# Plain products for the first two projections and the first output block, and other buffers around them, in a hybrid attention layer

## The chip, the cores and the metric

The kernel runs on one core of a Trainium2 chip. The core has engines that run side by side, each with its own queue of instructions that it takes strictly in order: TensorE (PE, matrix products; its weight loads are listed as PEld), VectorE (DVE), ScalarE (ACT), GpSimd (POOL) and SyncE (SP, which here only issues DMA transfers). Data move from the chip's main memory to SBUF by DMA; TensorE writes its sums to PSUM, which this kernel uses as eight banks of 128 x 512 fp32, each cut in two halves of 256 columns. The metric is device time in microseconds (us), lower is better.

## What is computed

One layer (`DEPTH = 1`) over 512 tokens with model width 2048, all in fp32:

```python
def reference(x, norm_g, w_in, q_norm_g, k_norm_g, rel_bias, w_out):
    h = rms_norm(x, norm_g)                                   # 512 x 2048
    proj = h @ w_in                                           # 512 x 8192
    qa, ka, va, ga, qb, kb, vb, gb = split(proj, 8 x 1024)
    ya = stick_breaking_attention(qa, ka, va)                 # 8 heads of 128
    yb = chunk_band_attention(qb, kb, vb, q_norm_g, k_norm_g, rel_bias)   # 8 heads of 128
    mixed = concat(ya * silu(ga), yb * silu(gb))              # 512 x 2048
    return x + mixed @ w_out
```

## The kernel before

**Units.** The first product (`h @ w_in`) is cut into 32 *units*: 8 groups of two heads (A groups: stick-breaking, B groups: chunk band), and for each group the four kinds q, k, v and gate. A unit is a 256 x 512 block of the projection, summed over the 2048 channels. The output product (`mixed @ w_out`) is cut into four blocks of 512 output columns, numbers 32 to 35 (`NU + q`), each in two halves `a = 0, 1` of the tokens.

**Seven products for eight.** Every block is a 2 x 2 block product. The kernel forms it with seven block products, Winograd's variant of Strassen's scheme: sums of weight blocks (s1 to s4), sums of token blocks (T1 to T4), seven products, and a combination afterwards. A block is built up in *steps*: a unit has four (each takes two channel blocks j, kk = 0 and 1), an output block has eight (one j each). A step of a unit is 7 x 2 x 3 = 42 matmuls, a step of an output block 7 x 2 halves x 3 = 42.

**Three matmuls for a product.** A fp32 value is split into a rounded high part and a remainder: ACT casts the high part (`xh`, `wh`, in fp32r), DVE subtracts it from the value (`xl`, `wl`). `three` (L374 to L376) then issues high x high, and the two mixed products.

**What comes ahead of a step.** Weights: `load` (L265) brings 512 KB by two transfers; `sums` makes s1 to s4 on DVE (L282 512 columns, L285 and L286 256 each); `split` casts on ACT (L298) and subtracts on DVE (L303) in two parts: part 0 is A11, s3, A12, A22 (1024 columns), part 1 is s1, s2, s4 (768). Each part has two buffers, so the cast for a step waits until the products of the step before last that use this part are done. Token blocks: `activations(j)` loads a block j and its partner (L341 to L343) into a home of two 128 x 1024 buffers, scales it by `norm_g` (L350), splits the raw 768 columns (L357, L358 with 768), forms T1 to T4 on DVE (L364, L366, L367) and splits them (L357, L358 with 1024). There are two homes: `cq`+`ck` for even j and `cv`+`cg` for odd j. They are also the buffers in which later the units' results q, k, v and gate lie. A home takes the next j only when all of this is done.

**The mixed heads.** The heads' results are stored to memory (`mixd`, L918) and staged again through the same two homes for the output product (L341 to L343 from `mixd`). In the second product the odd home (`cv`, `cg`) is free only when the last head's gate has been applied and stored, the even home when the last q and k have been read.

**Banks.** Units 2 to 31 rotate over banks 0 to 4, four banks each (`place`, `unit_banks`); unit 1 lies in banks 4 to 7. The output blocks use banks 0 to 3 for a = 0 and 4 to 7 for a = 1. Banks 5 to 7 (`SPARE`) serve the attention in between. A half of a bank may be written again when `combine` has read it: an ACT copy of the first two products to the tile `U` (L489), then DVE L508, L510, L513, L515, L530. There is one tile `U`, and `combine` holds it from L489 to L530.

**The order.** A planner in the program itself (`schedule`) writes down all instructions: it runs its own clock with an assumed cost for each instruction, and on each engine takes the ready instruction with the earliest due time. PE takes an attention step if one is ready, and else the next product of the list `program`. Its order is then fixed; on the chip every engine waits at the head of its queue for whatever its next instruction needs.

**Other names.** `R` (L649) is 1/rms of the tokens spread over partitions by eight small matmuls (L644); before, it is made in a spare bank that it gets when unit 1 has finished. `xs` (L612, L617) are the 16 loads and squares for it. `residual` adds x to an output tile by a POOL transfer and stores it; for the last block x is loaded ahead (`residual_load`, L570) and added on DVE (L524 to L526).

Of the kernel before, what the change touches and what calls it, by code (L numbers as in the profile page):

```python
# [36 lines left out]
ORDER = ("A11", "A12", "s3", "A22", "s2", "s1", "s4")  # L37
TOKENS = dict(A11=0, A12=1, s2=5, s3=4, s1=3, A22=6, s4=2)

PLACE = dict(A11=0, A12=1, s3=2, A22=3, s2=4, s1=5, s4=6)  # L40


SLOT = dict(A11=0, s3=1, A12=4, A22=5, s1=8, s2=9, s4=12)
# [4 lines left out]
def trunk_kernel(ctx: ExitStack, tc: tile.TileContext, xT, xn, wi, wqk, wo, ng, qg, kg, rel, out):  # L48

# [71 lines left out]
    class Op:  # L121
        def __init__(self, engine, cost, fn, due=None, lag=0.0):
            self.engine, self.cost, self.fn, self.lag = engine, cost, fn, lag
            self.due = due if callable(due) else (lambda d=clock[0] + LATE if due is None else due: d)
# [33 lines left out]
    def issue(engine, op):  # L158
        op.fn()
        busy[engine] = clock[0] + op.cost  # L160
        if engine == "SP":
            dma_free[0] = max(dma_free[0], clock[0] + op.cost) + op.lag / 330e3
            return dma_free[0] + 2.2
# [65 lines left out]

    for n, (u, r) in enumerate(steps_):  # L230
        if u < NU:
            put(n, 0, ORDER)
        elif u == NU and r < 2:

            if r == 0:
                for n_, a in ((n, 0), (n + 1, 0), (n, 1), (n + 1, 1)):
                    put(n_, a, ORDER)
        elif r == NJ - 1:
            for a in range(2):
                put(n, a, ORDER)  # L240
        else:
            for x in ORDER:
                for a in range(2):
                    put(n, a, (x,))
    at_part = {}
    for k, (n, x, a) in enumerate(program):
        at_part.setdefault((n, SLOT[x] // 8), k)
    last_use = {(n, SLOT[x] // 8): k for k, (n, x, a) in enumerate(program)}
    takes = [0.75 if steps_[n][0] < NU else 0.36 for n, x, a in program]
# [11 lines left out]
    def load(n):  # L261
        a, b = rows(n)
        t = wt_[n] = tmp([P, 14 * P], "wt", f"wt{n}", bufs=3)
        for i, x in enumerate((a, b)):
            sp.dma_start(t[:, 2 * i * H:2 * (i + 1) * H].rearrange("p (a b) -> p a b", b=H), x)  # L265
# [6 lines left out]
    def all_weights():  # L272
        for n in range(NS):
            yield lambda: n < 3 or ("split", n - 3, 0) in done and ("split", n - 3, 1) in done
            k0, k1 = at_part[n, 0], at_part[n, 1]
            yield Op("SP", 0.15, lambda: load(n), need(k0, 7), lag=P * 4096)
            spawn(sums(n, k0, k1), (0, n))
# [742 lines left out]
```

## Time and profile before

| | |
|---|---|
| median of 3 runs | 1028.09 us (1025.92 to 1030.35) |
| profiled execution | 1026.74 us, its span from first to last instruction 1025.0 us |
| granted TensorE clock, mean | 0.976 |
| PE busy | 938.8 us (92%), 7496 matmuls |
| DVE, ACT busy | 860.0 us (84%), 591.3 us (58%) |
| moved by DMA | 112.41 MB, mean 110 GB/s |

The profile lists for each engine when it was busy, what ended its idle times, and in which order things ran. A matmul's row has the modelled length of one matmul (about 0.28 us at full clock), while the next starts earlier; so a rate is read from a count over a stretch, not from the mean. The granted clock of a stretch is a share of full speed. The prediction cuts the execution into stages and reads each by what PE waited for there.

### The profile page before, as it was taken

The numbers are of one execution on the slowest core, as the hardware profiler recorded it, in microseconds if no ns is written. First come the engines' busy times: TensorE is split into PE (matmuls) and PEld (weight loads), VectorE is DVE, ScalarE is ACT, GpSimd is POOL, SyncE is SP. The second block draws the span as 40 slices with busy tenths as digits, with TensorE's granted clock in tenths as the row PEclk, the third lists the DMA queues.
The fourth block names the chain that finished last, engine by engine and source line by source line (L and its number), as shares of the span: only waits on it lengthen the run. The fifth ranks groups of instructions, "written<-read, shape, count | busy, mean of one in ns | idle before, by whom it ended". The sixth has DMA issues, their size and how long they took to land.

```text
span 1025.0 us, 19307 instructions
## 1 busy us (share of the span) xinstructions
PE 938.8 (92%) x7496; PEld 919.6 (90%) x7496; DVE 860.0 (84%) x1531; ACT 591.3 (58%) x1082; POOL 18.8 (2%) x61
## 2 busy tenths in 40 slices
PE   5689999999999999999999999999999839898996
PEld 4689999999999998999999899999999839798996
DVE  6999988888889878888898887989889958877764
ACT  8855774865467547745674675467577625333431
POOL 0000000000000000000000000000000000101000
PEclk9789999999999999999999999999999959999998
DMA  8632333223322332232233223322324344546361
GB/s 258 215 103 83 102 94 105 76 80 124 103 63 96 121 99 78 80 122 88 83 100 117 83 74 123 104 74 82 104 73 143 121 128 134 136 143 165 106 163 41
DMA packets 63883, 112.41 MB, mean 110 GB/s; under 512 B 7472, under 2 KB 11568, under 8 KB 63792
## 3 DMA queue, kind: packets, MB, share of 16 engines
q1 hardware_dynamic: 62064, 108.04, 32.9%
q0 software_dynamic: 1728, 3.15, 1.9%
q8 instruction: 58, 0.95, 0.4%
q14 instruction: 33, 0.27, 0.1%
HBM read 102.77 MB, written 8.39 MB: 108 GB/s over the span
## 4 chain that ended last, share of the span: by engine, by line
PE 74%; DVE 14%; ACT 5%; issue 3%; DMA 3%; SPq 1%; DVEq 0%; ACTq 0%
PE banks L374 24%; PE banks L375 23%; PE banks L376 23%; DVE wl L303 3%; ACT wh L298 2%; PE banks L838 2%; DVE U L513 2%; DVE wt L282 1%; DVE xl L358 1%; DMA wt<-in_wi 1%; PE banks L766 1%; DVE c L515 1%; DMA xcv<-in_xT 1%; ACT xh L357 1%; DVE wt L286 1%
## 5 line engine op out<-in xcount | busy, mean ns | idle before, releaser
L374 PE MATMUL banks<-xh,wh 128*128 128x256 f32 x1792 | 521.8, 291 | 32.4 <-ACT wh L298 11.8
L375 PE MATMUL banks<-xl,wh 128*128 128x256 f32 x1792 | 511.1, 285 | 8.4 <-DVE xl L358 8.4
L376 PE MATMUL banks<-xh,wl 128*128 128x256 f32 x1792 | 510.1, 285 | 1.0 <-DVE wl L303 1.0
L298 ACT CAST wh<-wt 128x1024 fp32r<-128x1024 f32 x320 | 300.6, 942 | 309.3 <-PE banks L375 171.3
L303 DVE TENSOR_TENSOR wl<-wt,wh 128x1024 fp32r<-128x1024 f32 x320 | 347.6, 1089 | 86.8 <-ACT wh L298 85.1
L374 PEld LDWEIGHTS banks<-xh,wh 128*128 128x128 f32 x1792 | 346.3, 193 | 39.4 <-DVE c L515 12.9
L375 PEld LDWEIGHTS banks<-xl,wh 128*128 128x128 f32 x1792 | 346.6, 193 | 10.4 <-DVE xl L358 10.1
L376 PEld LDWEIGHTS banks<-xh,wl 128*128 128x128 f32 x1792 | 346.5, 193 | 1.2 <-DVE wl L303 1.2
L374 PE MATMUL banks<-wh,xh 128*128 128x256 f32 x448 | 129.5, 289 | 30.0 <-ACT xh L357 15.0
L376 PE MATMUL banks<-wh,xl 128*128 128x256 f32 x448 | 128.7, 287 | 2.4 <-DVE xl L358 2.4
L282 DVE TENSOR_TENSOR wt<-wt 128x512 f32<-128x512 f32 x160 | 109.6, 687 | 25.0 <-DMA wt<-in_wo 16.2
L375 PE MATMUL banks<-wl,xh 128*128 128x256 f32 x448 | 128.3, 286 | 0.0
L374 PEld LDWEIGHTS banks<-wh,xh 128*128 128x128 f32 x448 | 87.6, 196 | 32.0 <-ACT xh L357 15.6
L376 PEld LDWEIGHTS banks<-wh,xl 128*128 128x128 f32 x448 | 87.5, 195 | 3.2 <-DVE xl L358 3.2
L375 PEld LDWEIGHTS banks<-wl,xh 128*128 128x128 f32 x448 | 87.7, 196 | 0.0
L285 DVE TENSOR_TENSOR wt<-wt 128x256 f32<-128x256 f32 x160 | 67.1, 421 | 2.2
L286 DVE TENSOR_TENSOR wt<-wt 128x256 f32<-128x256 f32 x160 | 67.3, 421 | 1.8
L489 ACT COPY U<-banks 128x512 f32<-128x512 f32 x40 | 23.2, 581 | 21.6 <-PE banks L376 13.7
L847 DVE TENSOR_TENSOR wtl<-banks,wth 128x128 fp32r<-128x128 f32 (+1 forms) x64 | 31.1, 486 | 4.0 <-ACT wth L846 3.6
L846 ACT CAST wth<-banks 128x128 fp32r<-128x128 f32 (+1 forms) x64 | 26.8, 423 | 10.8 <-POOL wtl L854 4.5
L838 PE MATMUL banks<-ident,W 128*128 128x128 f32 x160 | 28.4, 275 | 1.5 <-ACT W L744 1.2
L739 DVE TENSOR_TENSOR_SCAN W<-L,W 128x128 f32<-128x128 f32 (+3 forms) x32 | 26.3, 821 | 0.0
(123 smaller groups left out, 902.7 us busy)
## 6 DMA issues: line engine op xcount, KB each, us to landing
wt<-in_wi SPq DMA_DIRECT2D x256, 256.0 KB, 3.0
wt<-in_wo SPq DMA_DIRECT2D x64, 256.0 KB, 3.2
xs<-in_xn SPq DMA_DIRECT2D x16, 256.0 KB, 5.0
mixd<-c SPq DMA_DIRECT2D x16, 256.0 KB, 2.6
out<-co SPq DMA_DIRECT2D x16, 256.0 KB, 4.1
co<-in_xn POOLq DMA_DIRECT2D x12, 256.0 KB, 6.2
bias<-in_rel SPq DMA_DIRECT2D x8, 256.0 KB, 3.4
xcq<-in_xT SPq DMA_DIRECT2D x8, 128.0 KB, 3.3
```

The source lines that it names most:

```text
L282: yield DV(512, lambda: dve.tensor_tensor(out=some(t, 8, -7, 2), in0=some(t, 5, -5, 2), in1=some(t, 1, 0, 2), op=ALU.add), need(k0, 4))
L285: yield DV(256, lambda: dve.tensor_tensor(out=some(t, 9, 2), in0=some(t, 8, 2), in1=some(t, 0, 2), op=ALU.add), need(k1, 4))
L286: yield DV(256, lambda: dve.tensor_tensor(out=some(t, 12, 1), in0=some(t, 9, 2), in1=some(t, 4, 2), op=ALU.add), need(k1, 3.5))
L298: act.copy(x[0], t)
L303: yield DV(w, lambda: dve.tensor_tensor(out=l, in0=t, in1=h.bitcast(F32), op=ALU.subtract), need(k, 0.5))
L374: pe.matmul(o, lh, rh, start=start, stop=False, **kw)
L375: pe.matmul(o, lh, rl, start=False, stop=False, **kw)
L376: pe.matmul(o, ll, rh, start=False, stop=stop, **kw)
L739: yield Op("DVE", 0.08 + 2.1e-3 * w, lambda: dve.tensor_tensor_scan(out=W[:, ::-1], data0=L[:, ::-1], data1=W[:, ::-1], initial=0.0, op0=A ...
L838: pe.transpose(t[:, j * P:(j + 1) * P], src[:, j * P:(j + 1) * P], ident)
L846: yield AC(w, lambda: act.copy(th[:, blocks, :], tv))
L847: yield DV(w, lambda: dve.tensor_tensor(out=tl[:, blocks, :], in0=tv, in1=th[:, blocks, :].bitcast(F32), op=ALU.subtract))
```

## The change

Two tables replace the order and the placement: a step's products are now a list of (weight block, token block, target half). For units 0 and 1 (all four steps) and for output block 32 (all eight steps, `PLAIN_STEPS`), the list is `PLAIN`: the eight ordinary block products of the raw blocks. Such a block has four targets and two banks; its result needs no combination, only two ACT copies (`copied`). Its weights need no sums and no part 1. Weights of steps 0 and 1 are loaded and split in two halves.

Token block B12 is needed raw only for `PLAIN`; its split (`XB`, `xb`) lies in buffers that are idle at that time (`qk`, `wth`, `wtl`, `v`). The raw blocks are split in pieces (256, 256 for B12, 512 columns). Staging also makes T1 to T4 for the later blocks, in the same homes. For the mixed heads, odd j no longer wait for `cv` and `cg`: their home is the `qk` buffer, free when the last scores are done.

Output block 32 uses banks 4, 0 (a = 0) and 1, 3 (a = 1); the following ones 4, 0, 1, 2 and 3, 5, 6, 7. The second half's `combine` has a tile of its own (tag `bias`) in place of the shared `U`. `R` no longer waits for unit 1's banks. The loads of x for the last block (`residual_load`) come after step 1 of block 33 has begun. In the last block the store of the first half of the columns is spawned and no longer stands in the sequence. The planner's assumed costs of a product change a little (0.705 to 0.72, 0.355 to 0.36).

```diff
+WINOGRAD = (("A11", "B11", 0), ("A12", "B21", 1), ("s3", "T3", 2), ("A22", "T4", 3), ("s2", "T2", 4),
+            ("s1", "T1", 5), ("s4", "B22", 6))
+PLAIN = (("A11", "B11", 1), ("A11", "B12", 6), ("A21", "B11", 3), ("A21", "B12", 7),
+         ("A12", "B21", 1), ("A12", "B22", 6), ("A22", "B21", 3), ("A22", "B22", 7))
+ALONE = {1: 0, 6: 1, 3: 2, 7: 3}
+PLAIN_STEPS = 8
...
+    def plain(u, r):
+        return u < 2 or u == NU and r < PLAIN_STEPS
...
     for n, (u, r) in enumerate(steps_):
+        names = PLAIN if plain(u, r) else WINOGRAD
         if u < NU:
-            put(n, 0, ORDER)
-        elif u == NU and r < 2:
-            if r == 0:
-                for n_, a in ((n, 0), (n + 1, 0), (n, 1), (n + 1, 1)):
-                    put(n_, a, ORDER)
-        elif r == NJ - 1:
+            put(n, 0, names)
+        elif r in (0, NJ - 1):
...
+        if plain(*steps_[n]):
+            yield from split(n, 0, k)
+        else:
+            yield from sums(n, k, at_part[n, 1])
...
+        yield lambda: ((i < 1 or ("hi", having[part][i - 1], part) in done)
+                       and (i < 2 or position[0] > last_use[having[part][i - 2], part]))
...
         if mixed:
             g = j // 2 * 2
             yield lambda: (("store", g, j % 2) in done and ("store", g + 1, j % 2) in done
-                           and all(emptied(t_, NG - 1) for t_ in tags)
-                           and position[0] >= at_step[steps_.index((last, j // 2))] + NP)
+                           and position[0] > at_step[step_of[NU - 1, j // 2]] + 6)
+            yield lambda: all(emptied(t_, NG - 1) for t_ in STAGE[0]) if j % 2 == 0 else ("scores", 2 * NG - 1) in done
...
+        if mixed and j % 2:
+            rt = tmp([P, 2, 4 * H], "qk", f"x{j}{mixed}")
+            r, t = rt[:, 0, :], rt[:, 1, :]
...
+    def raw_split(j, mixed, r, k, x0, x1, names, h, l):
+        if h is None:
+            if mixed:
+                yield lambda: ("values", 2 * NG - 1) in done
+            h, l = xb(j, mixed)
+        s_ = r[:, x0 * H:x1 * H]
+        yield AC((x1 - x0) * H, lambda: act.copy(h, s_), need(k, 2.6))
+        yield DV((x1 - x0) * H, lambda: dve.tensor_tensor(out=l, in0=s_, in1=h.bitcast(F32), op=ALU.subtract), need(k, 0.5))
...
+    def unit_banks(u, a):
+        if alone(u):
+            return ((0, 1), (2, 3))[u] if u < NU else ((4, 0), (1, 3))[a]
+        if a:
+            return 3, 5, 6, 7
+        b = 4 * (sequence.index(u) - 1) if u < NU else 4
+        return [(b + i) % 5 for i in range(4)]
...
+    def copied(u, a):
+        v = view(u)
+        there = lambda *x: lambda: all(("product", u, y, a) in done for y in x)
+        c, t = yield from result(u, a)
+        for f, (x, y) in enumerate(((1, 6), (3, 7))):
+            yield there(x, y)
+            yield AC(512, lambda: act.copy(c[f], v(pair(u, a, x, y))), clock[0] + 1)
+            for z in (x, y):
+                del holder[place(u, a, z)]
+        yield from finish(u, a, t)
...
     def combine(u, a):
...
+        tag = "bias" if a else "U"
...
-        yield lambda: "U" not in done
-        done.add("U")
+        yield lambda: ("U", tag) not in done
+        done.add(("U", tag))
...
     def residual_load(a):
-        yield lambda: ("mix", NG - 1, 1) in done
+        yield lambda: position[0] >= at_step[step_of[NU + 1, 1]]
...
-    owner = {i: "unit 1" for i in SPARE}
+    owner = {}
```

**At the start, on DVE.** These are the first rows that DVE gets (behind a name stands a running number; `xcq00`, `xcv10` are blocks j = 0 and 1, `wt0`, `wt1` the weights of steps 0 and 1). Before:

```order
L364 TENSOR_TENSOR xck00_115<-xcq00_114 128x512
L366 TENSOR_TENSOR xck00_115<-xck00_115,xcq00_114 128x256
L358 TENSOR_TENSOR xl0_139<-xcq00_114,xh0_138 128x768
L367 TENSOR_TENSOR xck00_115<-xck00_115,xcq00_114 128x256
L282 TENSOR_TENSOR wt0_124<-wt0_124 128x2x2x128
L364 TENSOR_TENSOR xcg10_120<-xcv10_119 128x512
L358 TENSOR_TENSOR xl1_152<-xcv10_119,xh1_151 128x768
L366 TENSOR_TENSOR xcg10_120<-xcg10_120,xcv10_119 128x256
L285 TENSOR_TENSOR wt0_124<-wt0_124 128x2x128
L367 TENSOR_TENSOR xcg10_120<-xcg10_120,xcv10_119 128x256
L303 TENSOR_TENSOR wl0_0_159<-wt0_124,wh0_0_158 128x1024
```

After:

```order
L439 TENSOR_TENSOR xl0_115<-xcq00_112,xh0_114 128x256
L439 TENSOR_TENSOR xbqk0_148<-xcq00_112,xbqk0_148 128x256
L439 TENSOR_TENSOR xl1_119<-xcv10_116,xh1_118 128x256
L439 TENSOR_TENSOR xbqk0_148<-xcv10_116,xbqk0_148 128x256
L410 TENSOR_TENSOR xck00_113<-xcq00_112 128x512
L410 TENSOR_TENSOR xcg10_117<-xcv10_116 128x512
L344 TENSOR_TENSOR wl0_0_162<-wt0_128,wh0_0_161 128x512
L439 TENSOR_TENSOR xl0_115<-xcq00_112,xh0_114 128x512
L439 TENSOR_TENSOR xl1_119<-xcv10_116,xh1_118 128x512
L344 TENSOR_TENSOR wl0_0_162<-wt0_128,wh0_0_161 128x512
```

The sums over the weights (L282, L285) are gone, the raw splits stand first, and the weights' split comes in two halves, the first ahead of the larger token blocks.

**At the passage from the units to the output block, on SP's DMA queue.** `xcq..1` are mixed blocks in the even home, `xcv..1` (before) and `x..1` (after) those in the odd one; `wt131` and `wt132` are weights of output steps 3 and 4; the stores `mixd6` and `mixd7` come from the last two heads. Before:

```order
L341 DMA xcq41_9779<-mixd12_94 128x256
L342 DMA xcq41_9779<-mixd4_86 128x512
L343 DMA xcq41_9779<-mixd12_94 128x256
L265 DMA wt132_9786<-in_wo 128x512 x2
L918 DMA mixd6_88<-c31_9760 128x512
L918 DMA mixd7_89<-c31_9760 128x512
L570 DMA xres0_9828<-in_xn 128x512 x2
L570 DMA xres1_9831<-in_xn 128x512 x2
L341 DMA xcq61_9834<-mixd14_96 128x256
L342 DMA xcq61_9834<-mixd6_88 128x512
L343 DMA xcq61_9834<-mixd14_96 128x256
L341 DMA xcv11_9839<-mixd9_91 128x256
```

After:

```order
L406 DMA x11_9632<-mixd1_83 128x512
L281 DMA wt130_9681<-in_wo 128x512 x2
L281 DMA wt131_9723<-in_wo 128x512 x2
L401 DMA xcq21_9772<-mixd10_92 128x256
L402 DMA xcq21_9772<-mixd10_92 128x256
L406 DMA xcq21_9772<-mixd2_84 128x512
L401 DMA x31_9789<-mixd11_93 128x256
L402 DMA x31_9789<-mixd11_93 128x256
L406 DMA x31_9789<-mixd3_85 128x512
L281 DMA wt132_9817<-in_wo 128x512 x2
L1009 DMA mixd6_88<-c31_9801 128x512
L1009 DMA mixd7_89<-c31_9801 128x512
```

Blocks j = 1 and j = 3 stood behind the last heads' stores and the loads of x; now they stand ahead of the stores, and the loads of x follow much later.

**Between output blocks, on ACT.** The rows around the end of block 33; `U` is the copy of the first two products, once for a = 0 and once for a = 1, `wh0_145` the cast of the weights two steps on. Before:

```order
L298 CAST wh1_144_10734<-wt144_10589 128x768
L489 COPY U_10747<-banks_81 128x512
L298 CAST wh0_145_10783<-wt145_10645 128x1024
L298 CAST wh1_145_10796<-wt145_10645 128x768
L489 COPY U_10805<-banks_81 128x512
```

After:

```order
L340 CAST wh1_144_10780<-wt144_10639 128x768
L593 COPY U_10793<-banks_81 128x512
L593 COPY U_10825<-banks_81 128x512
L340 CAST wh0_145_10834<-wt145_10691 128x1024
```

The second copy follows the first directly, and writes another tile.

393 lines of the change are left out of this document (212 added, 181 removed).

## The prediction, made blind

> **What bounds the kernel now.** I read the whole execution by stages first: idle before PE's first matmul, units 0 and 1, units 2 to 31, the passage to the output product, the output product, the tail. The cuts are the first matmul (11.78), the 336th (76.60), and the last of the units and of the output. Columns are the stretch, its length, busy time and instructions of each engine, the granted clock, DMA share and rate.
>
> ```profile
> 0.00:11.78 11.78, 0.00 (x0) 0.00 (x0) 5.01 (x9) 8.74 (x14) 1.34 (x8) 1.00 0.72 225
> 11.78:76.60 64.82, 51.65 (x336) 48.71 (x336) 59.17 (x100) 47.15 (x85) 0.49 (x3) 0.87 0.58 187
> 76.60:816.00 739.40, 719.60 (x5824) 706.18 (x5822) 646.10 (x1193) 460.28 (x901) 6.25 (x38) 1.00 0.30 96
> 816.00:846.00 30.00, 9.90 (x41) 8.73 (x42) 18.86 (x31) 9.15 (x9) 0.00 (x0) 0.54 0.39 123
> 846.00:1015.60 169.60, 157.63 (x1300) 156.01 (x1298) 126.08 (x192) 65.36 (x73) 10.68 (x12) 1.00 0.45 128
> 1015.60:1025.00 9.40, 0.00 (x0) 0.00 (x0) 4.74 (x11) 0.59 (x1) 0.00 (x0) 0.71 0.30 112
> ```
>
> A matmul at full clock costs 157.63 / 1300 = 0.1213 us. So the 336 of units 0 and 1 are worth 40.8 us and took 64.8; the 41 of the passage are worth 5.0 and took 30. The middle is 97% PE, and its 19.8 us of idle time are small waits at each unit's end, which the change leaves as they are. The losses lie in the first, second, fourth and fifth stage. What PE waited for there, first until 77, then from 816 on (total, times, longest):
>
> ```profile
> PE banks L374 <- ACT wh L298: 11.8, 1, 11.8
> PE banks L375 <- DVE xl L358: 8.4, 7, 1.8
> PE banks L374 <- ACT xh L357: 3.8, 3, 1.6
> ...
> PE banks L374 <- ACT xh L357: 15.0, 2, 13.6
> PE banks L374 <- ACT U L489: 6.2, 3, 2.1
> PE banks L374 <- DVE co L515: 4.9, 3, 1.6
> ```
>
> At the start PE waits for split tokens, with DVE busy 59.17 of 64.82 us: DVE is the bound there. At the passage it waits 13.6 us for one block. Between output blocks it waits 11.1 us in three pairs, for `U` and for the banks behind it.
>
> **Start: what goes and comes.** In each of the eight steps DVE loses L282, L285, L286 and the 768 split, in the two units their combination. The DVE groups from 6 to 76 us:
>
> ```profile
> L303 DVE TENSOR_TENSOR wl<-wt,wh 128x1024 fp32r<-128x1024 f32 x10 | 12.2, 1220 | 0.7 <-ACT wh L298 0.6
> L303 DVE TENSOR_TENSOR wl<-wt,wh 128x768 fp32r<-128x768 f32 x9 | 8.6, 956 | 1.7 <-ACT wh L298 1.6
> L282 DVE TENSOR_TENSOR wt<-wt 128x512 f32<-128x512 f32 x11 | 7.4, 687 | 0.6 <-DMA wt<-in_wi 0.6
> L285 DVE TENSOR_TENSOR wt<-wt 128x256 f32<-128x256 f32 x11 | 4.5, 420 | 0.0
> L358 DVE TENSOR_TENSOR xl<-xcq,xh 128x768 fp32r<-128x768 f32 x4 | 3.8, 955 | 0.3 <-ACT xh L357 0.3
> ```
>
> By widths (1024: 1.22, 768: 0.96, 512: 0.69, 256: 0.42, for sums and splits alike): two blocks j and their two steps cost DVE 2 x (0.96 + 0.69 + 2 x 0.42 + 1.22) + 2 x (0.69 + 2 x 0.42 + 1.22 + 0.96) = 7.4 + 7.4 = 14.8 us before. After, no row shows a 256 split; I take the 0.42 of L285. Then 2 x (0.42 + 0.42 + 0.69 + 0.69 + 2 x 0.42 + 1.22) + 2 x 1.22 = 8.6 + 2.4 = 11.0 us. Before, the home of the odd j was loaded four times, every 16.5 us on average (first, second and last row below), each time when DVE had finished with it:
>
> ```profile
> 2.59 0.43 SPq L341 DMA_DIRECT2D xcv<-in_xT  x1
> 18.09 0.38 SPq L341 DMA_DIRECT2D xcv<-in_xT  x1
> 52.00 0.38 SPq L341 DMA_DIRECT2D xcv<-in_xT  x1
> 64.34 0.95 DVE L358 TENSOR_TENSOR xl<-xcv,xh 128x768 fp32r<-128x768 f32 x1
> ```
>
> The homes stay, T1 to T4 are still made in them before they are free, and TensorE gets 48 more matmuls, 5.8 us. So with DVE at 11.0 per pair the next limits decide: PE itself with 96 matmuls, 11.6 us; and ACT, whose queue also holds the scaling, the squares of `xs`, and a cast of weights that waits until the step before last is done, since plain steps use the part-0 buffers alone:
>
> ```profile
> 22.81 1.11 ACT L350 ACTIVATE xcq<-xcq,ng_t 128x256 f32<-128x256 f32 x2
> 26.08 0.72 ACT L350 ACTIVATE xcv<-xcv,ng_t 128x512 f32<-128x512 f32 x1
> 28.98 1.04 ACT L298 CAST wh<-wt 128x1024 fp32r<-128x1024 f32 x1
> 31.49 0.62 ACT L617 ACTIVATE xs<-xs 128x512 f32<-128x512 f32 x1
> ```
>
> Per pair ACT has 2 x (1.11 + 0.72) of scaling, casts of tokens of 2 x (2 x 0.55 + 0.62 + 1.04), by the nearest of these widths, 2 x 1.04 for weights and 4 x 0.62 for squares: 3.7 + 5.5 + 2.1 + 2.5 = 13.8 us. I take 15 per pair, with 1.2 for its waits. The first product starts sooner: no L282 (0.69), half a cast (0.5), and half the weights to land (about 1, an estimate from the 3.0 us of such a transfer in the page's list of issues): 9.6 in place of 11.78. Three more pairs put the last one at 54.6, its 96 matmuls end 11.6 later, `R`'s eight matmuls now stand within (1.05 us, 83.2 before), and PE goes cold twice:
>
> ```profile
> 28.18 0.38 PE L374 MATMUL banks<-xh,wh 128*128 128x256 f32 x1 [1.58 <-ACT xh L357]
> 29.70 0.54 PE L375 MATMUL banks<-xl,wh 128*128 128x256 f32 x1 [1.14 <-DVE xl L358]
> 30.00:32.00 2.00, 2.00 (x11) 2.00 (x11) 1.84 (x3) 2.00 (x5) 0.00 (x0) 0.50 0.77 254
> 34.00:36.00 2.00, 2.00 (x19) 2.00 (x19) 1.85 (x4) 0.98 (x3) 0.00 (x0) 1.00 0.95 277
> 83.21 1.05 PE L644 MATMUL banks<-diag,ones 128*128 128x128 f32 x8
> ```
>
> After these two waits the clock stands at 0.50 and only 11 matmuls start in 2 us, not the 19 (two of them cut by the edges) at 1.00: a cold spell of 3 to 4 us costs 1.5 to 2. With two of them, 54.6 + 11.6 + 1.05 + 3.5 = 70.8; I take **71 for the end of unit 1, against 76.6: -5.6**. Bounds: PE never waits, 9.6 + 384 x 0.1213 + 3 (cold at first) + 1.05 = 60.2; nothing gained from DVE, the last operand at 65.2 as before and 96 matmuls behind it, 76.9. 71 is nearer the second, because ACT's 13.8 is near the old cycle. The Trainium skill (TensorE: Matmul & The Clock Gate, "What's actually happening") says that the clock halves after an idle window of about 3.4 us; by that only the gap ahead of the second pair would be cold, and the end about 69. The row (0.50 after two waits of 1.58 and 1.14 us between lone matmuls) speaks for counting shorter gaps too.
>
> **Units 2 to 31.** Same products, banks and weights: 739.4 less the 1.05 of `R` = 738.4. The DVE relief buys nothing here.
>
> **The passage.** Before, the last gate's chain held the odd home:
>
> ```profile
> 818.77 0.69 DVE L515 TENSOR_TENSOR c<-banks,U 128x512 f32<-128x512 f32 x1
> 824.92 1.29 DVE L912 TENSOR_TENSOR c<-c,c 128x512 f32<-128x512 f32 x2
> 825.63 0.93 SPq L918 DMA_DIRECT2D mixd<-c  x2
> 826.66 1.86 SPq L570 DMA_DIRECT2D xres<-in_xn  x4
> 829.98 0.51 SPq L341 DMA_DIRECT2D xcv<-mixd  x1
> 835.86 0.95 DVE L358 TENSOR_TENSOR xl<-xcq,xh 128x768 fp32r<-128x768 f32 x1
> 836.65 0.58 PE L374 MATMUL banks<-wh,xh 128*128 128x256 f32 x1 [13.57 <-ACT xh L357]
> ```
>
> Block j = 1 could be loaded only behind the stores at 825.6 and the 1 MB of x, and PE stood until 836.65. Now j = 1 is loaded into `qk` during the last unit. Only j = 6 and 7 need the last heads. Ahead of them lie six steps of 16 products, 6 x 48 x 0.1213 = 34.9 us of PE work: j = 6 is wanted at 851, and its raw part stood ready at 836.8 before. That covers the chain by 14 us. Banks: a = 0 starts in bank 4, idle, and bank 0, freed by the early copy L489; a = 1 wants bank 1, freed by L515 of the last unit, at 819.5 before, 3.5 after the units' end, and a = 0 gives 24 x 0.1213 = 2.9 us of work. So a wait of under 1 us there. Next late is DVE. From the last unit's L508 (now L600) to the weights of output step 2 it has in line, by widths, the unit's combination 2.6, the gate's three multiplies 2.6, the raw splits of j = 2 and 3 with 3.1, their sums 3.1 and two weight splits 2.4: 13.8 us, begun a little before the units' end, and step 2 is wanted 11.6 us after it. I charge 2 us for this and the bank, with 0 and 12 as bounds: 12 if DVE enters that list with a backlog of 10.
>
> **Output blocks.** 96 more matmuls in the kernel, 48 of them here, 5.8 us. Between the blocks before:
>
> ```profile
> 883.86 0.59 ACT L489 COPY U<-banks 128x512 f32<-128x512 f32 x1 [0.94 <-DVE co L530]
> 884.50 0.38 PE L374 MATMUL banks<-wh,xh 128*128 128x256 f32 x1 [2.13 <-ACT U L489]
> ```
>
> The copy for a = 1 waited for L530 of a = 0 because both use `U`, PE waited for the copy and then, by the list of waits, for L515: 11.1 / 3 = 3.7 us each time. With a tile of its own the copy runs as soon as its two products are there, some 4 us sooner; 3 x 0.5 us is left for L513 and L515 behind other DVE work. At the first boundary ACT's copies of 0.59 replace the chain altogether.
>
> So from 816: 1389 matmuls x 0.1213 = 168.5, passage 2, boundaries 1.5, and 0.9 as before (169.6 - 157.6 - 11.1): **172.9 against 199.6, -26.7**. Bounds 169.5 and 185.
>
> **Tail.** The second half's copy waited for L530 here too:
>
> ```profile
> 1016.71 0.59 ACT L489 COPY U<-banks 128x512 f32<-128x512 f32 x1 [4.83 <-DVE co L530]
> ```
>
> Now both halves' DVE rows mix; their sum is the same, only the copy's 0.6 and its hand-over leave the chain: 8.4 against 9.4, **-1** (0 to 1.5).
>
> **Sum.** 71.0 + 738.4 + 172.9 + 8.4 = 990.7 against 1025.0: -34.3. The profiled execution took 1026.74 and would take 992.4; the median lies 1.35 above it, so I forecast **993.8 us**.
>
> **Rivals.**
> (1) The start gives nothing (17%). ACT's in-order queue takes DVE's place: a cast of weights stands in it ahead of the next pair's scaling and waits for PE, so PE and ACT wait for each other in turn. For it: ACT at 13.8 per pair, and a cycle of 16.5 before. Against: 47.15 of 64.82 busy before, and its work grows little. Then 76.9, +5.9: 999.7.
> (2) The passage is only half filled (10%): DVE is late with step 2's weights and the raw splits. For it: DVE busy 18.86 of 30 there before, while it worked off the last unit. Against: the sums for eight output steps (2.5 us each) are gone. 12 in place of 2: 1004.
> (3) The boundaries stay as they are (3%), because L513 and L515 of a = 1 stand behind weight splits in DVE's queue: +9.6, 1003.
> (4) Everything is hidden (8%): start at 60.2, from 816 169.5, tail 7.9: 979.
> (5) Slower (4%). One part of the weights, two buffers: each of the 16 plain steps would expose the cast and split (1.04 + 1.22) and the operands behind them in ACT's queue, in place of the 5.8 us that PE gives them now. At 2.5 us a step it costs 40 us on top of a start and passage that gain 34: about 1034 with the waits that stay. It decides from 34.3 / 16 = 2.1 us a step. Against it: a step is 48 matmuls long, and the cast needs only the step before last.
>
> **How the numbers follow.** Forecast 58%, itself 985 to 1000. The rivals (1), (2), (3) end at 999.7 to 1004, (4) at 979. I give 982 to 1006, which leaves out (5), most of (4) and the worst of (2) with (1). A measurement of this kernel can tell about 0.5%, 5 us, from no change. All cases but (5) are beyond that: faster 0.94, within 0.02 (several rivals at once), slower 0.04.
>
> **What would show it.** Right: unit 1's last matmul near 71, ACT and no longer DVE ahead of PE's waits there; no PE wait over 3 us after the units' end and the clock at 1.00 there; waits for L593 (the new `U` copy) under 1 us a time; 7592 matmuls; the middle at 738 within 3. Wrong: a second matmul of the start later than 11, a pair cycle of 16 or more, clock 0.50 after the units, PE waiting for `wl` in plain steps, or a middle that grows, which would mean that PE was not its bound.

## The result

The changed kernel takes **986.52 us** (median of 4 runs, 984.94 to 987.2) against 1028.27 us (1025.92 to 1030.35) for the kernel before, run beside it: a ratio of 0.9592, 95% interval 0.9569 to 0.9616. The forecast was 993.8 us, with a range of 982 to 1006. A later batch with five rounds gave 987.48 us and 0.9609 (0.9596 to 0.9622).

The profiled execution took 986.68 us, span 984.9 us, mean clock 0.993. These are its stages, in the same columns as before: idle, units 0 and 1 (384 matmuls and `R`'s eight), units 2 to 31, the output product, the tail.

```profile
0.00:10.16 10.16, 0.00 (x1) 0.00 (x1) 2.92 (x7) 7.13 (x15) 1.35 (x8) 1.00 0.67 209
10.16:70.10 59.94, 54.17 (x392) 52.65 (x393) 47.12 (x87) 46.13 (x95) 0.62 (x3) 0.94 0.66 211
70.10:805.80 735.70, 718.46 (x5810) 704.39 (x5809) 638.66 (x1190) 460.15 (x906) 6.32 (x38) 1.00 0.30 97
805.80:976.00 170.20, 167.87 (x1394) 167.19 (x1392) 130.62 (x201) 73.77 (x91) 10.69 (x12) 1.00 0.52 150
976.00:984.90 8.90, 0.14 (x2) 0.00 (x0) 5.03 (x12) 0.00 (x0) 0.00 (x0) 0.63 0.32 118
```

Line numbers are new: the three matmuls are L444 to L446, a weight cast and its subtraction L340 and L344, those of a raw token piece L438 and L439, scaling L427, token loads L401 to L406, the combination L593 (copy to `U`) to L611; an experiment with added lines moves them on by some.

The fourth stage is nearly all PE: 1392 matmuls and 2.3 us of waiting. The granted clock stands at 1.00 in it; before, the 30 us from 816 on had 0.54. Over the whole execution PE waited for (total, times, longest):

```profile
PE banks L444 <- DVE c L605: 10.7, 14, 1.2
PE banks L444 <- ACT wh L340: 10.2, 1, 10.2
PE banks L444 <- DVE c L600: 5.0, 5, 1.1
PE banks L444 <- ACT xh L438: 4.4, 3, 2.4
PE banks L444 <- DVE co L605: 2.3, 2, 1.1
PE banks L445 <- DVE xl L439: 1.3, 2, 0.9
```

Gone are the 13.6 us for block 1 and every wait for the copy to `U`. The second row is the idle time ahead of the first matmul; the fourth and the sixth are what is left of the start's waits; the others are small waits at the ends of units and output blocks.

The units' end of before must be cut more exactly than the prediction did: its first output matmul stands at 814.76, and its last at 1015.4. By these cuts, each in us:

| stage | before | after | change | predicted change |
|---|---|---|---|---|
| to the end of units 0, 1 | 76.6 | 70.1 | -6.5 | -5.6 |
| units 2 to 31 | 738.1 | 735.7 | -2.4 | -1.05 |
| output product | 200.6 | 170.2 | -30.4 | -26.7 |
| tail | 9.6 | 8.9 | -0.7 | -1 |
| span | 1025.0 | 984.9 | -40.1 | -34.3 |

### The profile page after: what moved, and what is told of

It is laid out like the page before. It is cut to its first block, busy times and chain, and to the rows that moved or that the text cites. A ratio compares the mean times of both kernels' runs of the same rounds, so it can differ in the third digit from the quotient of the medians.

```text
span 984.9 us, 19439 instructions
## 1 busy us (share of the span) xinstructions
PE 940.6 (96%) x7592; PEld 924.2 (94%) x7592; DVE 824.4 (84%) x1493; ACT 587.2 (60%) x1104; POOL 19.0 (2%) x61
## 4 chain that ended last, share of the span: by engine, by line
PE 80%; DVE 10%; ACT 4%; DMA 3%; issue 2%; SPq 0%; DVEq 0%; ACTq 0%
PE banks L444 26%; PE banks L445 25%; PE banks L446 25%; DVE wl L344 4%; ACT wh L340 3%; DMA wt<-in_wi 2%; PE banks L929 2%; DVE U L604 1%; PE banks L857 1%; DVE wt L320 1%; DVE c L605 1%; PE banks L965 1%; DVE c L600 0%; PE banks L802 0%; DVE wt L323 0%
## 5 line engine op out<-in xcount | busy, mean ns | idle before, releaser
L444 PE MATMUL banks<-xh,wh 128*128 128x256 f32 x1776 | 514.3, 290 | 30.3 <-DVE c L605 10.7
L445 PE MATMUL banks<-xl,wh 128*128 128x256 f32 x1776 | 503.9, 284 | 1.4 <-DVE xl L439 1.3
L446 PE MATMUL banks<-xh,wl 128*128 128x256 f32 x1776 | 503.5, 283 | 0.0
L340 ACT CAST wh<-wt 128x1024 fp32r<-128x1024 f32 (+2 forms) x306 | 287.5, 942 | 278.2 <-PE banks L445 168.4
L344 DVE TENSOR_TENSOR wl<-wt,wh 128x1024 fp32r<-128x1024 f32 (+2 forms) x306 | 331.7, 1088 | 91.5 <-ACT wh L340 88.3
L444 PEld LDWEIGHTS banks<-xh,wh 128*128 128x128 f32 x1776 | 341.0, 192 | 36.6 <-DVE c L605 13.5
L446 PEld LDWEIGHTS banks<-xh,wl 128*128 128x128 f32 x1776 | 341.2, 192 | 0.2 <-DVE wl L344 0.2
L444 PE MATMUL banks<-wh,xh 128*128 128x256 f32 x432 | 122.6, 284 | 2.3 <-DVE co L605 2.3
L446 PE MATMUL banks<-wh,xl 128*128 128x256 f32 x432 | 122.2, 283 | 0.0
L320 DVE TENSOR_TENSOR wt<-wt 128x512 f32<-128x512 f32 x144 | 98.3, 685 | 27.6 <-DMA wt<-in_wi 14.9
L444 PEld LDWEIGHTS banks<-wh,xh 128*128 128x128 f32 x432 | 82.9, 192 | 2.9 <-DVE co L605 2.7
L446 PEld LDWEIGHTS banks<-wh,xl 128*128 128x128 f32 x432 | 82.9, 192 | 0.0
L324 DVE TENSOR_TENSOR wt<-wt 128x256 f32<-128x256 f32 x144 | 60.2, 419 | 2.3
L323 DVE TENSOR_TENSOR wt<-wt 128x256 f32<-128x256 f32 x144 | 60.0, 418 | 1.8
L593 ACT COPY U<-banks 128x512 f32<-128x512 f32 x36 | 21.0, 583 | 19.7 <-PE banks L446 19.7
L835 ACT ACTIVATE W<-W 128x128 f32<-128x128 f32 (+3 forms) x32 | 15.0, 470 | 18.6 <-DVE W L833 18.6
```

What stands on the lines that cost most here:

```text
L320: yield DV(512, lambda: dve.tensor_tensor(out=some(t, 8, -7, 2), in0=some(t, 5, -5, 2), in1=some(t, 1, 0, 2), op=ALU.add), need(k0, 4))
L323: yield DV(256, lambda: dve.tensor_tensor(out=some(t, 9, 2), in0=some(t, 8, 2), in1=some(t, 0, 2), op=ALU.add), need(k1, 4))
L324: yield DV(256, lambda: dve.tensor_tensor(out=some(t, 12, 1), in0=some(t, 9, 2), in1=some(t, 4, 2), op=ALU.add), need(k1, 3.5))
L340: act.copy(whl[n, part][0][:, c], t)
L344: yield DV(c.stop - c.start, lambda: dve.tensor_tensor(out=l[:, c], in0=t, in1=h[:, c].bitcast(F32), op=ALU.subtract), need(k, 0.5))
L444: pe.matmul(o, lh, rh, start=start, stop=False, **kw)
```

## The experiments

All of them edit the changed kernel. Each gives the median, its range and the ratio to the kernel before with its 95% interval. The three parts of the output side, taken away one at a time, give back 13.0, 5.6 and 3.6 us of the 31 that the last two stages gained; the other 9 were not assigned. The later loads of x and the new banks were not taken away by themselves.

**1. One tile `U` for both halves.**

```diff
-        tag = "bias" if a else "U"
+        tag = "U"
```

> The changed kernel, with one tile U for both halves of the tokens again. Theory (the shared U made PE wait between output blocks): the first boundary stays empty, since the plain block has no combination and so no U; at the two others the second half's copy waits for the first half's last row again and PE for 3.7 us in place of 1.1, and the tail is 0.7 longer: 986.5 + 2 x 2.6 + 0.7 = about 992.5. Rival (the other banks did it, a block begins in a bank that is free): no copy of the second half has anything behind it that PE wants, 986 to 987.5.

Measured: 992.09 us (990.49 to 992.92), ratio 0.9656 (0.9637 to 0.9676), so 5.6 us more. The output product takes 175.3 us, +5.1, the tail 9.5, +0.6. PE's wait at the boundary after block 33 in the order of time, changed kernel:

```profile
897.08 0.39 PE L444 MATMUL banks<-wh,xh 128*128 128x256 f32 x1 [1.14 <-DVE co L605]
```

and the stretches (columns as above) on both sides of it:

```profile
892.00:898.00 6.00, 4.86 (x40) 4.66 (x40) 5.97 (x12) 1.59 (x2) 2.39 (x3) 1.00 0.49 81
898.00:904.00 6.00, 6.00 (x52) 6.00 (x51) 4.69 (x8) 2.94 (x3) 1.12 (x2) 1.00 1.02 224
```

With one `U`, in the order of time (the third row is the tail's copy):

```profile
894.46 0.59 ACT L593 COPY U<-banks 128x512 f32<-128x512 f32 x1 [0.81 <-DVE co L604]
898.43 0.58 PE L444 MATMUL banks<-wh,xh 128*128 128x256 f32 x1 [2.35 <-DVE co L605]
982.47 0.59 ACT L593 COPY U<-banks 128x512 f32<-128x512 f32 x1 [4.83 <-DVE co L604]
```

and the stretch behind the wait:

```profile
898.00:904.00 6.00, 5.57 (x36) 5.57 (x37) 2.27 (x4) 1.88 (x2) 1.77 (x2) 0.73 0.96 222
```

The copy again waits for the last row of the other half, and PE for 2.35 us in place of 1.14. The rest of the loss is the clock: after the longer wait its mean over six microseconds is 0.73, and from 898.43 to 904 only 36 matmuls start where full clock gives 5.57 / 0.12 = 46, 1.2 us. So a boundary costs 1.2 + 1.2 = 2.4 us more, two of them 4.8, and the tail 0.6. The theory holds; the banks alone do not do it.

**2. The odd home of before.**

```diff
-            yield lambda: all(emptied(t_, NG - 1) for t_ in STAGE[0]) if j % 2 == 0 else ("scores", 2 * NG - 1) in done
+            yield lambda: all(emptied(t_, NG - 1) for t_ in STAGE[j % 2])
...
-        if mixed and j % 2:
+        if False:
```

> The changed kernel, with the odd mixed blocks staged through cv and cg again, as before; they can be loaded only when the last gate has been stored. Theory (the home is what filled the passage): block 1 comes as late as before, 20 us after the units' end; block 0 now gives PE 48 matmuls, 5.8 us, so PE waits some 13 us there and is cold for 2 more: about 1001. Rival (the plain products, which need no sums on DVE, filled it): at most 3 us more, 987 to 989.5.

Measured: 999.5 us (998.81 to 1001.03), ratio 0.9733 (0.9713 to 0.9752), 13.0 more. The load of block 1 and PE's wait for it, in the order of time:

```profile
819.29 0.38 SPq L401 DMA_DIRECT2D xcv<-mixd  x1
823.66 0.58 PE L444 MATMUL banks<-wh,xh 128*128 128x256 f32 x1 [10.70 <-ACT xh L438]
```

and the stretches before, in and behind the wait:

```profile
806.80:813.00 6.20, 6.16 (x50) 5.79 (x48) 6.17 (x13) 2.65 (x3) 0.00 (x0) 1.00 0.28 88
813.00:823.60 10.60, 0.00 (x0) 0.00 (x0) 5.21 (x9) 5.32 (x9) 0.00 (x0) 0.60 0.60 199
823.60:830.00 6.40, 6.29 (x32) 5.99 (x33) 5.62 (x11) 2.92 (x5) 0.00 (x0) 0.59 0.27 70
```

In the changed kernel the same block is loaded into `qk` during the last unit:

```profile
790.88 0.33 SPq L401 DMA_DIRECT2D x<-mixd  x1
```

With the old home PE does block 0 (50 matmuls in the first row, all 6.2 us busy), stands for 10.7 us, and runs the next 6.4 us at a mean clock of 0.59, 32 matmuls where 53 would fit, 2.5 us. 10.7 + 2.5 = 13.2: the home is what the passage hung on.

**3. Seven products for eight in the output block, wholly or in its second half.**

```diff
-PLAIN_STEPS = 8
+PLAIN_STEPS = 0
```

> The changed kernel, with seven products for eight in the first output block too; units 0 and 1, homes, banks and tiles stay as changed. 48 matmuls fewer, 5.8 us. Theory (DVE is the next one late at the passage): the sums of eight weight steps, 2.5 us each, and the combination come back to DVE, which then delivers the weights and token blocks of the first output steps late: PE waits 8 to 12 us and goes cold behind it, 990 to 996. Rival (the odd home alone fills the passage and DVE keeps up): 5.8 less and 2 for one more boundary, about 983.

Measured: 990.12 us (989.84 to 990.72), ratio 0.964 (0.9622 to 0.9658). With `PLAIN_STEPS = 4`:

> The changed kernel, with plain products in only the first four of the first output block's eight steps, seven products for eight in the other four, with a combination. 24 matmuls fewer, 2.9 us. Theory (DVE has 7 us to spare from 821 to 860 and gets four times 2.5 us of sums and the combination of the block back, so PE waits again for a part of it): 985 to 988. Rival (only the passage itself needs DVE free): 2.9 less, 983.5.

Measured: 989.23 us (987.0 to 990.71), ratio 0.9624 (0.9601 to 0.9647). Both edits change more than the expectations say: block 32 then ends with a combination, so it takes the banks 4, 0, 1, 2 and 3, 5, 6, 7 in place of 4, 0 and 1, 3, and a third boundary has a combination ahead of it. The first run does 48 matmuls fewer and is 3.6 us slower; its output product takes 174.4 us, so 4.2 + 5.8 = 10.0 us of other losses stand against the saved work. The granted clock is 1.00 over this stage, so none of it is the cold clock that the theory expected too:

```profile
805.26:979.60 174.34, 164.34 (x1346) 161.92 (x1344) 143.35 (x228) 74.96 (x88) 10.70 (x12) 1.00 0.51 144
```

PE waits 10.0 us here in place of 2.3. Of the 7.7 more, 2.1 are one wait for a bank that the last unit's combination frees, 3.5 are six waits for split weights and tokens, and 2.1 lie at the boundaries; the rest are smaller gaps between matmuls. The first of these waits, and the longest for a split:

```profile
808.95 0.39 PE L444 MATMUL banks<-wh,xh 128*128 128x256 f32 x1 [2.09 <-DVE c L605]
848.74 0.39 PE L446 MATMUL banks<-wh,xl 128*128 128x256 f32 x1 [1.00 <-DVE xl L439]
```

The stretches from 821 to 860 of the run without plain products there:

```profile
821.00:836.00 15.00, 13.95 (x112) 13.36 (x112) 15.00 (x26) 7.32 (x10) 0.00 (x0) 1.00 0.52 163
836.00:860.00 24.00, 20.03 (x158) 19.01 (x158) 24.00 (x43) 11.24 (x14) 2.79 (x3) 1.00 0.45 123
```

of the changed kernel:

```profile
821.00:836.00 15.00, 15.00 (x127) 15.00 (x126) 12.21 (x21) 8.46 (x14) 0.00 (x0) 1.00 0.70 219
836.00:860.00 24.00, 24.00 (x202) 24.00 (x201) 19.36 (x29) 12.36 (x17) 3.67 (x4) 1.00 0.50 124
```

With the sums back, DVE is busy 39 of 39 us and PE starts 270 matmuls in place of 329. Here eight products are cheaper than seven: the saved product is paid on DVE, which is short of time, and in banks that are not yet free. With four plain steps DVE is again busy 39 of 39, and the output product takes 171.8 us with 24 matmuls fewer, so 4.5 us of other losses. But PE waits for no split weight or token in this run. It waits for a bank at the passage (with the granted clock at 1.00 around it, second row), and 1.4 us more than the changed kernel at the boundaries:

```profile
807.74 0.36 PE L444 MATMUL banks<-wh,xbwth 128*128 128x256 f32 x1 [2.66 <-DVE c L605]
805.00:811.00 6.00, 3.34 (x28) 3.29 (x28) 5.96 (x12) 3.46 (x7) 0.00 (x0) 1.00 0.59 194
```

The same row of DVE in the changed kernel:

```profile
808.18 0.68 DVE L605 TENSOR_TENSOR c<-banks,U 128x512 f32<-128x512 f32 x1
```

It ends there at 808.86, 3.0 us after the first output matmul (805.83), and in the run with four plain steps 3.0 us after it, too (807.59 and 804.56). The bank does not come later, PE wants it sooner: after 3 matmuls, where the two banks of a plain block let it run 24. So in both runs DVE ends the waits, but "late with the weights and token blocks" covers only 3.5 us of the first and nothing of the second, which also came out above its bounds by 1 us; the rival, 983.5, failed as well. No run has the sums with two banks or plain products with four, so the shares of sums and banks are not separated further.

**4. What makes the start shorter.** Four runs take its parts away. First the plain products of units 0 and 1 (with banks, combination and undivided weight loads to match):

```diff
-        return u < 2 or u == NU and r < PLAIN_STEPS
+        return u == NU and r < PLAIN_STEPS
...
-    owner = {}
+    owner = {i: "unit 1" for i in SPARE}
```

> The changed kernel, with seven products for eight in units 0 and 1, in banks 0 to 3 and 4 to 7 with a combination, and undivided weight loads; the token blocks are still loaded and split in the smaller pieces, and the output side stays as changed. Theory (DVE's sums and splits set the start, and the plain products took them away): unit 1 ends 7 to 8 us later, 994. Rival (the smaller pieces of tokens, which let the first product of a step begin earlier, made the gain): at most 2 us later, 986.5 to 988.5.

Then the pieces of tokens at the start, once with plain products and once with seven for eight (a token block and its partner in one load, the raw 768 columns split at once, B12 apart where it is needed):

```diff
-        spawn(raw(j, mixed, Op("SP", 0.08, lambda: sp.dma_start(r[:, H:3 * H], b), need(k, 9), lag=P * 2048), r, k + 4,
-                  [(1, 3, ("B21", "B22"), f(h[:, 1:3]), f(l[:, 1:3]))], j + NJ, not mixed), (0, 0, j))
...
+            spawn(raw_whole(j, Op("SP", 0.2, all_three, need(k, 10), lag=P * 4096), r, k,
+                            [(0, 3, ("B11", "B21", "B22"), f(h[:, :3]), f(l[:, :3]))] + [(3, 4, ("B12",), None, None)]), (0, 0, j))
```

> The changed kernel, plain products kept, but at the start a token block and its partner are loaded as one step and the first 768 columns are cast and subtracted in one instruction each, as before. With both at the start undone but these pieces kept the time had come to 990.3, 3.8 more, where the whole start gains 7.7. Theory (two causes that add up: plain products some 3, the pieces some 4.5): 990 to 991.5. Rival (the pieces matter only where DVE is the bound, and plain products have removed that): 986.5 to 988.

> The changed kernel with seven products for eight in units 0 and 1, undivided weight loads and undivided token blocks at the start: the start of before in products and in pieces, the output side as changed. Theory (nothing else of the change shortens the start): unit 1 ends at about 76.6 as before, 986.5 + 7.7 = 994 to 995. Rival (the gain that is left without plain products came from the planner's order and due times, not from the pieces): as with the pieces, 990 to 991.

Last, on top of the third, due times, the order of transfers and the loading of weights one after the other as before:

```diff
-            yield AC((x1 - x0) * H, lambda: act.activation(s_, s_, AF.Copy, scale=ng_t[:, c_:c_ + 1]), need(k, 3.5))
+            yield AC((x1 - x0) * H, lambda: act.activation(s_, s_, AF.Copy, scale=ng_t[:, c_:c_ + 1]), need(k, 7))
...
-        yield lambda: n == 0 or ("loading", n - 1) in done
+        yield lambda: n == 0 or (("landed" if n < 9 else "loading"), n - 1) in done
```

> The kernel of the run with seven products and undivided token blocks at the start (990.1), and now also the due times of token loads, scaling, casts and splits, the order of the three transfers and the one-after-the-other loads of weights as before, so that the rows stand on SP, ACT and DVE nearly as before. That run had unit 1 at 72.8, not at 76.6: neither products nor pieces explain the last 4 us of the start's gain. Theory (the order of rows does: before, the sums of tokens stood ahead of the raw splits that PE wanted first): 993 to 995. Rival (another part, such as the rule for the homes): 990 to 991.

Measured, with the end of units 0 and 1 in each profile; where `R`'s eight matmuls (1.05 us) come after it, they are added, so that all rows hold the same work:

| start | end of unit 1 + `R` | median us | ratio (95%) |
|---|---|---|---|
| changed kernel | 70.1 | 986.52 | 0.9592 (0.9569 to 0.9616) |
| seven products | 73.6 | 990.31 | 0.9644 (0.9622 to 0.9667) |
| plain products, whole blocks | 75.2 | 993.37 | 0.9667 (0.9645 to 0.9688) |
| seven products, whole blocks | 73.9 | 990.12 | 0.9639 (0.9619 to 0.9659) |
| the same, order of before | 75.3 | 991.35 | 0.9651 (0.9638 to 0.9664) |
| kernel before | 77.7 | 1028.27 | 1 |

(The profile with plain products and whole blocks also loses 1.4 us in units 2 to 31, that with seven products and whole blocks 1.4 in the output product; the ends of unit 1 are the cleaner measure.) Six profiles with the start of the changed kernel (it twice, and experiments 1 to 3) end unit 1 between 69.3 and 70.4, so about 1 us between two rows can be chance. None of the four theories held; of the rivals, that of the third run did (990 to 991). Pieces make no difference with seven products (73.6 and 73.9) and 5.1 us with plain ones. Plain products without pieces are worse than seven, by 1.3 us at the end of unit 1 and by 3.2 in the median, whose ranges do not overlap (992.62 to 993.98 and 989.9 to 992.19). The two do not add up; each is worth something only with the other. With seven products and pieces PE's waits up to the end of unit 1 end mostly with DVE's splits of tokens (9.0 us in 5 waits); with plain products and whole blocks they end mostly with ACT's casts (7.0 us in 3). Smaller casts can shorten only the latter. That this is why the pieces matter only there is argued from these waits, not shown by a further run. Two of the three, the first product of the second pair of token blocks and the first in the third pair that needs the pair's second block:

```profile
28.59 0.39 PE L461 MATMUL banks<-xh,wh 128*128 128x256 f32 x1 [4.00 <-ACT xh L455]
47.97 0.38 PE L461 MATMUL banks<-xh,wh 128*128 128x256 f32 x1 [2.29 <-ACT xh L455]
```

They wait for the cast of three quarters of a block (768 columns), which stands behind the loads and the scaling of these columns. In the changed kernel a cast of 256 columns is enough (the rows at 26.89 and 43.64 are the same two products):

```profile
26.89 0.38 PE L444 MATMUL banks<-xh,wh 128*128 128x256 f32 x1 [2.38 <-ACT xh L438]
28.91 0.39 PE L444 MATMUL banks<-xh,wh 128*128 128x256 f32 x1 [1.06 <-ACT xh L438]
43.64 0.38 PE L444 MATMUL banks<-xh,wh 128*128 128x256 f32 x1 [0.96 <-ACT xh L438]
```

Taken away in this order, of the 7.6 us 3.5 go with the plain products, 0.3 with the pieces and 1.4 with the order of rows (73.9 to 75.3). The 1.4 is little more than chance: the two medians, 990.12 and 991.35, have overlapping ranges. Another 2.4 (75.3 to 77.7) are left in the last run, whose rows stand on SP, ACT and DVE nearly as before. What gives these was not found.

**5. The 16 loads of xs.** The second pair in the changed kernel, first and last load on SP, then ACT, in the order of time:

```profile
16.93 0.56 SPq L401 DMA_DIRECT2D xcq<-in_xT  x1
22.09 0.33 SPq L406 DMA_DIRECT2D xcv<-in_xT  x1
18.72 1.05 ACT L340 CAST wh<-wt 128x1024 fp32r<-128x1024 f32 x1 [1.47 <-PE banks L445]
23.14 0.51 ACT L427 ACTIVATE xcq<-xcq,ng_t 128x256 f32<-128x256 f32 x1 [0.96 <-DMA xcq<-in_xT]
24.48 1.04 ACT L340 CAST wh<-wt 128x1024 fp32r<-128x1024 f32 x1 [0.83 <-PE banks L445]
```

and the stretch around it:

```profile
18.00:24.00 6.00, 6.00 (x53) 6.00 (x52) 1.79 (x2) 3.52 (x8) 0.00 (x0) 1.00 1.03 372
```

The token blocks are issued from 16.93 to 22.09 among loads of xs, the DMA engines are full (share 1.03), ACT waits for the block, and DVE is idle for 4.2 of these 6 us. So load number i of xs was held back:

```diff
             for i in range(4):
+                yield lambda: position[0] >= 8 + 3 * (4 * t + i)
                 k, = yield from buffer("W")
                 spawn(x_stat(t, i, k), (0, 1))
```

> The changed kernel, with the 16 loads and squares of xs for the norm spread out: load number i is held back until product 8 + 3 i has been planned. Theory (the pair cycle of 16.7 us at the start is set by transfers and ACT, where xs takes 4 MB and 10 us of ACT): the cycle drops to about 15 and unit 1 ends 2 to 3 us earlier, 983.5 to 985. Rival (the cycle is set by the casts of weights that wait for TensorE, with two buffers): no change, 986 to 987.5.

Measured: 982.91 us (982.39 to 984.46), ratio 0.9567 (0.9548 to 0.9586). Since it beat the changed kernel, both were run again on one chip, with a third that holds xs back further (`40 + 4 * (4 * t + i)`):

> The changed kernel itself, to be set beside the two that follow on the same chip: 986.5.

> The changed kernel with the loads and squares of xs spread over units 0 and 1, a second time beside the changed kernel. Theory (transfers and ACT at the start): 3 to 4 us less than the changed kernel, 983. Rival (chance of one batch): within 1 us of it.

> The same with load number i held back until product 40 + 4 i, so that most of xs comes after unit 1. Theory (xs is in the way of the token loads as long as these run, until about 50 us): the start gains 1 to 2 us more, 981 to 982.5. Rival (R then comes late, all heads behind it, and the middle grows by what the start gains): 983 to 986.

Measured: 987.48 us (985.93 to 988.06), ratio 0.9609 (0.9596 to 0.9622); 983.2 us (980.08 to 984.25), 0.9568 (0.9551 to 0.9585); 992.29 us (991.63 to 993.44), 0.9663 (0.965 to 0.9676). In the profile of the second the same two loads read:

```profile
14.56 0.43 SPq L401 DMA_DIRECT2D xcq<-in_xT  x1
17.82 0.33 SPq L406 DMA_DIRECT2D xcv<-in_xT  x1
```

and its second and third stage:

```profile
9.50:65.10 55.60, 51.34 (x384) 49.45 (x385) 42.85 (x72) 45.06 (x94) 0.65 (x3) 0.97 0.70 229
65.10:802.40 737.30, 719.89 (x5818) 705.37 (x5817) 642.14 (x1206) 460.54 (x906) 6.34 (x38) 1.00 0.29 96
```

The blocks are issued by 17.82 in place of 22.09. The second pair's first product, 26.89 in the changed kernel, comes at

```profile
22.75 0.28 PE L444 MATMUL banks<-xh,wh 128*128 128x256 f32 x1
```

and unit 1 ends at 65.1 (`R` follows). The edit also moves ACT's squares of xs; their part is not separated from that of the transfers. This version beats both kernels, by 4.3 us or 0.4% the changed one, and the intervals of the batch do not overlap. The third shows the price of going on; its middle stage

```profile
64.70:810.80 746.10, 722.34 (x5819) 707.67 (x5818) 642.29 (x1203) 465.80 (x927) 6.88 (x41) 1.00 0.30 99
```

and, in the order of time, `R`:

```profile
103.09 1.06 PE L737 MATMUL banks<-diag,ones 128*128 128x128 f32 x8
```

Unit 1 ends sooner still, at 64.7, but `R` comes at 103 and all heads behind it, and the middle grows by 746.1 - 735.7 = 10.4 us. The rival held, with a larger price than it named.

## Why the prediction was right, and where it was not

The forecast was 7.3 us too high, with 41.8 us of gain where it had 34.3; sign, order of the parts and range held. By its steps:

- **Start, 71.0 forecast, 70.1 measured: the sum held, its cause only in part.** The first product came at 10.16 (9.6 forecast), those of the second to fourth pair at 26.89 (above) and

```profile
42.16 0.28 PE L444 MATMUL banks<-xh,wh 128*128 128x256 f32 x1
58.45 0.28 PE L444 MATMUL banks<-xh,wh 128*128 128x256 f32 x1
```

  That is a cycle of 16.1 on average, and the prediction had named 16 or more as a sign of being wrong. But the three cycles, 48.3 us, hold the two cold spells and `R` within them, and the forecast had these on top of three times 15: 45 + 3.5 + 1.05 = 49.6. The last 96 matmuls took 11.7 (11.6 forecast). So the errors are small, and two of opposite sign cancel in part. PE's waits end mostly with ACT's casts, as said (4.4 of 5.7 us). That ACT's 13.8 us of work per pair set the cycle is not shown: ACT was busy 46.13 of 59.94 us and DVE 47.12, and at the second pair ACT itself waited first for the transfer (0.96 above) and then for PE (0.83). Experiment 5 moved the token loads ahead of xs and took 1.9 us out of the start in its first run and 4.2 in its second (67.2 and 65.1, each with 1.05 for `R`, against 70.1 and 70.4). The casts that wait for PE (1.47 and 0.83 above) are rival (1)'s mechanism; it is there, and did not eat the gain. (The old cycle of 16.5 us is read from the three loads among the prediction's rows, the last of which is no load.)
- **The credit for it was misplaced.** The prediction put the start's gain down to DVE's relief and treated the splits in pieces as a detail of cost. Experiment 4 gives plain products 3.5 of 7.6, and only together with the pieces; 1.4, little more than chance, go with the order of rows; 2.4 stay open.
- **Two cold spells, 3.5 us.** The granted clock shows two in the changed kernel, behind the second and the third pair's waits, and the sum's size fits, but no run here takes one away alone. The 3 us "cold at first" in the lower bound were about 2.7: the first 24 matmuls took 5.6 us, where 24 x 0.1206 is 2.9.
- **Units 2 to 31, -1.05 forecast, -2.4 measured.** `R` moved out as said. The other 1.3 was not separated; without `R` this stage took 734.1 us in the run with the order of before at the start and 736.1 with one `U`, though neither edits it, so 1 us either way says nothing.
- **Passage, 2 us forecast, 0 measured.** The mechanism is shown: with the old home 13 us come back. The list of DVE work ahead of step 2 was right, and the margin was nil, so that PE did not wait there was luck. Two rows of DVE in the changed kernel, the splits of the weights for steps 2 and 6:

```profile
816.20 1.22 DVE L344 TENSOR_TENSOR wl<-wt,wh 128x1024 fp32r<-128x1024 f32 x1
836.26 1.22 DVE L344 TENSOR_TENSOR wl<-wt,wh 128x1024 fp32r<-128x1024 f32 x1 [1.18 <-ACT wh L340]
```

  Step 2 is wanted 2 x 48 matmuls after 805.83, at 817.4, and its split ends at 817.42. Step 6 is wanted at 840.5 and ready at 837.5: 3 us, where the prediction had a cover of 14. It did not count the weights, and it took the time of block 6's raw split, 20.8 us after the units' end, from the kernel before; now this split ended 28.9 us after it (834.74). Rival (2) was nearer than 10% says, for nothing was in hand at step 2. Experiment 3 does not show that it would have ruled: with four steps' sums back PE waits for no split, with all eight for 3.5 us.
- **Boundaries, 1.5 us forecast, 2.3 measured.** 0.5 each was too little for the two with a combination (1.14 each), and 0.5 too much for the first, which has none. Experiment 1 confirms `U`. Rival (3) is refuted: 2.3 us in place of 11.1.
- **The rate.** 1392 matmuls took 170.2 - 2.3 = 167.9 us, 0.1206 each, not 0.1213: 1 us. The 0.1213 probably held some small waits, which the prediction counted again as 0.9 of rest. These two, the passage and the boundaries are about the 2.7 us by which the output product beat the forecast of 172.9.
- **Tail, 8.4 forecast, 8.9 measured.** Only the copy's 0.6 went (9.5 with one `U`).
- **The median** lay 1.35 us above the profiled execution before and 0.2 below it now; the prediction carried the 1.35 over.
- **Rival (5)** is refuted: the first two units got shorter, and in the output block plain steps are the faster ones.

## What to carry to other kernels

Seven products for eight save a tensor engine time only while the engines that form the sums have time to spare and the banks of the larger result are free; at the start, at a passage or wherever operands are late, the plain product can be the faster one, but only if its first operands arrive in pieces small enough for it to begin. Where a stage waits, look also at what stands ahead of its loads in the queue: transfers that nobody needs yet, with the work behind them on ACT, cost this start 2 to 4 us, and held back too far they cost 10 us later. Two changes that look separate can be worth nothing apart, so take them away singly and together.

## What the runs showed of the hardware

A wait of 1.14 us between two output blocks left the granted clock at 1.00 in the six microseconds behind it; one of 2.35 us (experiment 1) brought its mean to 0.73 there and cost 1.2 us beyond the wait itself; one of 10.70 us brought 0.59 and 2.5 us. But the length of a wait did not decide alone: one of 2.66 us (experiment 3, four plain steps) left the clock at 1.00. The Trainium skill (TensorE: Matmul & The Clock Gate, "What's actually happening") puts the fall at an idle window of about 3.4 us. The wait of 2.66 us agrees with that, the one of 2.35 us does not; what tells them apart no run here shows. On this kernel's evidence a wait of over 2 us may cost some clock, and is to be counted with a range.

The clock column does not show the slow spell at the very start. In the changed kernel

```profile
12.00:14.00 2.00, 2.00 (x11) 2.00 (x11) 1.40 (x4) 2.00 (x7) 0.00 (x0) 1.00 0.90 288
```

has 11 matmuls in 2 us, as the prediction's row with a clock of 0.50, while its column says 1.00. So at the start a rate is read from the count of matmuls.
